# RWKV-7 and Mamba-2 hybrid step: the chunk products of two heads issued in turn, on one Trainium2 core

## The chip, the cores and the metric

The kernel runs on one core of one Trainium2 chip. The metric is device time in microseconds (us). A core has TensorE (PE, with its weight loads shown apart as PEld), VectorE (DVE), ScalarE (ACT), GpSimd (POOL) and SyncE (SP, which here issues the DMAs); each works off its own list of instructions in order, and they meet through semaphores. PSUM, where TensorE writes, has eight banks.

## What is computed

One layer of a streaming encoder for 512 prompt frames (with 16 learned tokens ahead of them) and 64 frames of a running stream, width 2048. Half of the projected columns feed RWKV-7 with 16 heads of 64, the other half Mamba-2; then an output projection, a SwiGLU feed-forward part and a final norm. Cut to the part that matters here:

```python
h = rmsnorm(x, norm_mix_w)
proj = (h @ w_in).astype(F32)
ya, ... = rwkv7_mix(proj[..., :A_COLS], ...)      # r, k, v, decay, a per head of 64
yb, ... = mamba2_mix(proj[..., A_COLS:], ...)
x = x + jnp.concatenate([ya, yb], axis=-1).astype(dtype) @ w_out
h2 = rmsnorm(x, norm_ffn_w)
x = x + (jax.nn.silu(h2 @ ffn_w_gate) * (h2 @ ffn_w_up)) @ ffn_w_down

def step(S, inp):                                 # RWKV-7, one time step
    r_t, w_t, k_t, v_t, kk_t, ka_t = inp
    sa = jnp.einsum('bhij,bhj->bhi', S, kk_t)
    S = S * w_t[:, :, None, :] - sa[..., None] * ka_t[:, :, None, :] + v_t[..., None] * k_t[:, :, None, :]
    return S, jnp.einsum('bhij,bhj->bhi', S, r_t)
```

The kernel doesn't run the recurrence step by step. It cuts time into 10 chunks of 64. In a chunk, products between the (decayed) keys and queries of the 64 steps are taken first, a triangular system is solved, and only a short chain over the chunks is left. The products between keys and queries are what the change is about.

## The kernel before

Work is written out in full when the program is built. A main stream issues the projection as tiles of 128 columns (`in_tile`, line 367, through `product`, line 326): 16 blocks of 128 rows, three products each (high and low halves of the weights) for two halves of the columns of time. Everything else is a task, a Python generator: `go` (206) puts it on a list by priority, and `beat` (215), called three times in each block of the main stream, lets every task go one step whose time has come. Times come from a planner inside the kernel: each engine call is wrapped (`Timed`, 149) and adds an estimated duration to that engine's clock (`tick`, 136). So the order of the instructions on every engine is fixed at build time, by these costs; on the chip only semaphores count. A `yield "P"` gives the turn back until TensorE's time has come, `"VA"` until DVE and ACT are free too.

The 16 heads of RWKV are taken as eight pairs j. The two heads of a pair lie in rows 0 to 63 and 64 to 127 (`hrow`). Per pair:

- `pre_k` and `pre_r` (743, 789) build `KB` and `ST`, from which the gram products are taken. `pre_k` takes two banks of its own for row sums (tile `ss`).
- In `pre_r` (lines 811 to 819) the gram products follow: for each head, for groups of 4, 4 and 2 chunks (`groups`, 787), one bank is taken with `get` (250), one product per chunk goes to it (64 rows, 128 columns out, 128 columns moving, fp32), and `gram_out` (770) is put on the list with priority `PRG` = 1. Tile names begin with `gr`.
- `gram_out` reads one bank: two masked multiplications on DVE, four copies on ACT, then `put` gives the bank back.
- With all six groups read, POOL solves the triangular system in 62 operations (31 steps); `steps` (855) transposes `KB`; `solved` and `applied` (880, 918) apply the solution (tiles `pm`, `pb`, `px`). The gram products of the next pair wait for the `px` products of this one.
- `chain` (984) runs over the 10 chunks (tile `p`, bank 4, priority 0), `post` (1034) normalises.

The tasks of this stage share banks 5, 6 and 7 (line 604 leaves these); the main stream has 0 to 3.

Of the kernel before, what the change touches and what calls it, by code (L numbers as in the profile page):

```python
# [11 lines left out]
F32R = mybir.dt.float32r  # L12
# [5 lines left out]
P = 128  # L18
# [59 lines left out]
PRG = 1  # L78
# [8 lines left out]
def tile_hybrid(ctx, tc, xt, wq, wg, wd, lrw, cst, vec, s0w, s0m, y_out, sh_out, wkv_out, cv_out, sm_out):  # L87
    nc = tc.nc
    V, A, G, PE, SY = nc.vector, nc.scalar, nc.gpsimd, nc.tensor, nc.sync
# [28 lines left out]
    def bank(i, name):  # L118
        return psp.tile([P, 512], F32, tag=f"b{i}", name=name)
# [16 lines left out]
    def tick(e, us):  # L136
        c = cur[0]
        if c.eng != e:
            c.eng, c.base = e, c.t + (0.17 if e == "PE" and c is not main else 0.0)
        end = max(free_at[e], c.base) + us  # L140
        free_at[e] = c.last = end
        if c is not main and not c.aside:
            c.t = max(c.t, end + 0.2)
# [5 lines left out]
    class Timed:  # L149
# [5 lines left out]
        def __getattr__(self, op):  # L155
            f, e = getattr(self.eng, op), self.e

            def call(out, *a, **k):
                r = f(out, *a, **k)  # L159
                part = 0.1 * (out.shape[0] <= 64)  # L160
                if e == "PE":
                    n = out.free_size()
                    tick(e, n / 2400 + 0.0133 if a[1].dtype == F32R else 0.175 if op == "transpose" else max(0.218, 0.15 + n / 1100))
                else:
                    n = (a[0] if op == "tensor_reduce" else out).free_size()
                    s = table.get(a[1]) if op == "activation" else None
                    if s and s != table["now"]:
                        table["now"] = s
                        tick(e, 1.28)
                    if e == "V" and op == "transpose":  # L170
                        us = 0.07 + n / (540 if n > 1000 else 720)
                    elif e == "V" and op in ("tensor_tensor_scan", "reciprocal"):
                        us = 0.07 + n / (480 if op == "tensor_tensor_scan" else 155)
                    elif e == "V":
                        fast = op in ("tensor_copy", "tensor_scalar") and a[0].space == out.space
                        us = 0.07 + n / (960 if not fast else 1920 if not part else 1400) + part * (n > 64)
                        us += 0.06 * (op in SCALED and not isinstance(a[1], float))
                    elif e == "A":
                        us = 0.06 + part + n / 1090 + 0.11 * any(not isinstance(q, float) for q in k.values())
                    else:  # L180
                        us = (0.35 if n < 128 else 0.25) + n / (475 if op == "tensor_tensor" else 1000)
                    tick(e, us)
                return r

            return call

    V, A, G, PE = Timed(V, "V"), Timed(A, "A"), Timed(G, "G"), Timed(PE, "PE")
# [18 lines left out]
    def go(g, prio=5):  # L206
        t = Step()
        t.t, t.g, t.prio = max(now(), cur[0].t), g, prio
        tasks.append(t)
        tasks.sort(key=lambda t: t.prio)  # L210

    def mark(key):
        done[key] = now() if cur[0] is main else cur[0].t
# [14 lines left out]
    def until(*keys, then=None):  # L228
        for k in keys:
            while k not in done:  # L230
                yield then
            cur[0].t = max(cur[0].t, done[k])
        if cur[0].t > now() + SLACK[2]:
            yield then
# [15 lines left out]
    def get():  # L250

        while not spare:
            yield "P"
        b, t = spare.pop(0)
        cur[0].t = max(cur[0].t, t)
        if cur[0].t > now() + SLACK[2]:
            yield "P"
        return b

    def put(b):  # L260
        spare.append((b, cur[0].last + 0.2))
# [410 lines left out]
    R, ses, MVs, st_o = {}, [], [], []  # L672
    hrow = [slice(0, 64), slice(64, 128)]
# [96 lines left out]
    def gram_out(j, h, c0, n, b, pg):  # L770

        yield "VA"
        gb_, st, kx = R["GB"], R["ST"][j % 2][h], 64 * h
        q, m = vrow[h], cc("m3")[:, 64 - 64 * h:192 - 64 * h]
        bc = lambda a: a.unsqueeze(1).broadcast_to([64, n, a.shape[1]])
        V.tensor_tensor(st[q, c0:c0 + n], pg[q, 0:n], bc(m[q]), ALU.mult)
        q, rr = hrow[h], slice(64 - kx, 128 - kx)
        V.tensor_tensor(gb_[q, c0:c0 + n, rr], pg[q, 0:n, rr], bc(m[q, rr]), ALU.mult)
        lo, hi = slice(kx, kx + 32), slice(kx + 32, kx + 64)
        A.copy(R["NX"][lo, c0:c0 + n, :], pg[lo, 0:n, lo])  # L780
        A.copy(R["NX"][hi, c0:c0 + n, :], pg[hi, 0:n, hi])
        A.copy(R["NS"][lo, c0 // 2:(c0 + n) // 2, hi], pg[lo, 0:n:2, hi])
        A.copy(R["NS"][hi, c0 // 2:(c0 + n) // 2, lo], pg[lo, 1:n:2, hi])
        put(b)
        mark(("gram", j, h, c0))

    groups = [(0, 4), (4, 4), (8, 2)]

    def pre_r(j):

        E3 = Eb[:, 0:650].rearrange("p (c t) -> p c t", t=CH + 1)
        Em3 = Em[:, 0:650].rearrange("p (c t) -> p c t", t=CH + 1)
        yield from until("low", ("prek", j), ("Tm", j - 1), then="V")
        KB = R["KB"]
        for h in range(2):
            q, kx = hrow[h], 64 * h
            V.tensor_tensor(KB[q, :, kx:kx + 64], c3(ab)[q], Em3[q, :, 1:CH + 1], ALU.mult)
            yield "V"
            V.tensor_tensor(KB[q, :, 64 - kx:128 - kx], c3(k2)[q], Em3[q, :, 1:CH + 1], ALU.mult)
            yield "V"  # L800
        yield from until(("zr", j), ("cl", j - 2), then="V")
        for h in range(2):
            q, kx, st = hrow[h], 64 * h, R["ST"][j % 2][h]
            V.tensor_tensor(st[q, :, kx:kx + 64], c3(rn)[q], E3[q, :, 0:CH], ALU.mult)
            yield "V"
            V.tensor_tensor(st[q, :, 64 - kx:128 - kx], c3(zr)[q], E3[q, :, 1:CH + 1], ALU.mult)
            yield "V"
        mark(("kb", j))
        go(bonus(j), 2)
        yield from until(*[("px", j - 1, g) for g in range(3)], then="P")  # L810
        for h in range(2):
            q, st = hrow[h], R["ST"][j % 2][h]
            for c0, n in groups:
                b = yield from get()
                pg = bank(b, f"gr{j}{h}{c0}").rearrange("p (c x) -> p c x", x=P)
                for c in range(c0, c0 + n):
                    PE.matmul(pg[:, c - c0, :], KB[q, c, :], st[q, c, :], start=True, stop=True)
                go(gram_out(j, h, c0, n, b, pg), PRG)
                yield "P"
        go(steps(j), PRG)  # L820
        yield from until(*[("gram", j, h, c0) for h in range(2) for c0, _ in groups], then="A")
        mark(("gram", j))

        NX, NN, XT = R["NX"], R["NN"], R["XT"]
        for g in range(1, 3):
            A.copy(NX[:, 10 * g:10 * g + 10], NX[:, 0:10])
        X3 = R["XX"][:, 0:352].rearrange("p (i t) -> p i t", t=32)
        yield "V"
        yield from until(*[("px", j - 1, g) for g in range(3)], then="V")
        V.transpose(NN, NX.rearrange("p c t -> p t c"))  # L830
        yield "P"
        for s in range(31):
            m, r = 31 - s, s // 3 + 1
            tv = XT[:, 0:r * m].rearrange("p (i t) -> p i t", t=m)
            G.tensor_tensor(tv, X3[:, 0:r, s:s + 1].broadcast_to([P, r, m]),
                            NN[:, s + 1:32, s].unsqueeze(1).broadcast_to([P, r, m]), ALU.mult)
            G.tensor_tensor(X3[:, 0:r, s + 1:32], X3[:, 0:r, s + 1:32], tv, ALU.subtract)
        mark(("solve", j))
        yield "P"
        go(solved(j), PRG)  # L840
# [306 lines left out]
    for j in range(NPAIR + 1):  # L1147
        if j < NPAIR:
            go(decay(j), 3)
            go(pre_k(j), 3)  # L1150
            run(f"k{j}", shift_k(j), 1)
            run(f"r{j}", shift_r(j), 1)
        for i in PARK[j]:
            run(f"z{i}", park(i), 1)
        if j < NPAIR:
            go(pre_r(j), 2)
            go(values(j), 2)
            go(chain(j), 0)
        if j:
            run(f"v{j - 1}", shift_v(j - 1), 1)  # L1160
# [834 lines left out]
    for h in range(2):  # L1995
        go(last_norm(h), 2)
        for o in range(NK):
            ps = slot(3, f"e{h}{o}")
            hs = LHS[h]
            x = [[(a[:, hs], c[:, hs]) for a, c in (XT[k] for k in range(4))]]  # L2000
# [161 lines left out]
```

## Time and profile before

| | us |
|---|---|
| median of 3 runs | 2800.07 |
| lowest and highest | 2793.95, 2803.86 |
| the profiled execution | 2797.02 |
| its span, first to last instruction | 2795.1 |
| PE, DVE, ACT, POOL busy | 2658.5, 2187.0, 1405.9, 385.8 |

An fp32 product is shown as two MATMUL records with a weight load each, so the 160 gram products are 320 records. Tiles are named without their numbers: `gr` are the gram banks, `mk`, `mr`, `mv`, `mz`, `mB`, `mC`, `mx` the tiles of the projection. Nearly all lines read L159, since every engine call goes through one helper. "Chain" is the chain of work that ended last, followed back from the end of a stretch. PEclk is the granted clock of TensorE as a share of its upper level.

### The profile page before, as it was taken

The numbers are of one execution on the slowest core, as the hardware profiler recorded it, in microseconds if no ns is written. First come the engines' busy times: TensorE is split into PE (matmuls) and PEld (weight loads), VectorE is DVE, ScalarE is ACT, GpSimd is POOL, SyncE is SP. The second block draws the span as 40 slices with busy tenths as digits, with TensorE's granted clock in tenths as the row PEclk, the third lists the DMA queues.
The fourth block names the chain that finished last, engine by engine and source line by source line (L and its number), as shares of the span: only waits on it lengthen the run. The fifth ranks groups of instructions, "written<-read, shape, count | busy, mean of one in ns | idle before, by whom it ended". The sixth has DMA issues, their size and how long they took to land.

```text
span 2795.1 us, 51964 instructions
## 1 busy us (share of the span) xinstructions
PE 2658.5 (95%) x19236; PEld 2587.9 (93%) x19236; DVE 2187.0 (78%) x4216; ACT 1405.9 (50%) x3013; POOL 385.8 (14%) x673
## 2 busy tenths in 40 slices
PE   8998899989999999989999999999999979999897
PEld 8888789989998989989999999999999979989897
DVE  7675787878778674678988888898888668878785
ACT  5645566556655443454445445444544334444344
POOL 3234324444401110220000000000000000000004
PEclk9999799999999999999999999999999989999899
DMA  5421122222122244343434344443434666373523
GB/s 180 173 74 50 47 70 65 69 57 77 56 86 91 97 150 122 119 150 121 150 128 158 129 144 144 141 150 128 158 128 150 211 213 207 117 229 95 182 76 110
DMA packets 196462, 349.57 MB, mean 125 GB/s; under 512 B 26097, under 2 KB 102001, under 8 KB 196081
## 3 DMA queue, kind: packets, MB, share of 16 engines
q1 hardware_dynamic: 196208, 346.26, 38.6%
q8 instruction: 151, 2.47, 0.4%
q14 instruction: 103, 0.84, 0.1%
HBM read 281.13 MB, written 65.06 MB: 124 GB/s over the span
## 4 chain that ended last, share of the span: by engine, by line
PE 77%; DVE 5%; ACT 4%; DMA 4%; POOL 3%; issue 2%; SPq 0%; DVEq 0%; ACTq 0%; POOLq 0%
PE y L159 14%; PE a L159 14%; PE r L159 14%; PE x L159 7%; PE mwo L159 7%; DVE mem L159 5%; POOL mem L159 3%; PE mx L159 3%; ACT mem L159 3%; PE mv L159 3%; PE mk L159 2%; PE mr L159 2%; DMA ffm<-pd 2%; PE mz L159 2%; PE p L159 2%
## 5 line engine op out<-in xcount | busy, mean ns | idle before, releaser
L159 ACT CAST memr<-mem 128x512 fp32r<-128x512 f32 (+2 forms) x1230 | 714.3, 585 | 925.3 <-PE y L159 210.0
L159 DVE TENSOR_TENSOR memr<-mem,memr 128x512 fp32r<-128x512 f32 (+2 forms) x1076 | 692.3, 648 | 282.5 <-ACT memr L159 275.4
L159 DVE TENSOR_TENSOR mem<-mem 128x576 f32<-128x576 f32 (+9 forms) x1016 | 695.8, 701 | 36.0 <-DMA mem<-x1d 26.1
L159 POOL TENSOR_TENSOR mem<-mem 128x84 f32<-128x84 f32 (+28 forms) x583 | 337.1, 579 | 2256.0 <-ACT mem L159 1591.0
L159 ACT ACTIVATE mem<-mem 64x64 f32<-64x64 f32 (+12 forms) x413 | 217.0, 533 | 175.1 <-DVE mem L159 155.5
L159 PE MATMUL r<-ffm,memr 128*128 128x288 f32 x1348 | 206.0, 299 | 17.3 <-DVE memr L159 12.7
L159 PE MATMUL a<-ffm,memr 128*128 128x288 f32 x1328 | 201.9, 299 | 12.5 <-ACT memr L159 9.9
L159 PE MATMUL mwo<-memr 128*128 128x288 f32 x1536 | 210.4, 298 | 0.0
L159 PE MATMUL y<-ffm,memr 128*128 128x288 f32 x1356 | 203.4, 297 | 7.2 <-DMA ffm<-pd 7.2
L159 PE MATMUL y<-memr 128*128 128x288 f32 x1352 | 203.0, 296 | 6.5 <-DVE mem L159 5.5
L159 PEld LDWEIGHTS mwo<-memr 128*128 128x128 f32 x1536 | 205.9, 189 | 3.0 <-issue 2.5
L159 PEld LDWEIGHTS r<-ffm,memr 128*128 128x128 f32 x1348 | 190.5, 192 | 19.5 <-DVE memr L159 13.0
L159 PE MATMUL x<-memr 128*128 128x288 f32 x1352 | 201.5, 295 | 0.0
L159 PE MATMUL a<-memr 128*128 128x288 f32 x1352 | 200.3, 295 | 1.2 <-DVE memr L159 1.2
L159 PEld LDWEIGHTS a<-ffm,memr 128*128 128x128 f32 x1328 | 187.1, 191 | 14.2 <-ACT memr L159 10.1
L159 PE MATMUL r<-memr 128*128 128x288 f32 x1352 | 199.1, 294 | 0.0
L159 PEld LDWEIGHTS y<-ffm,memr 128*128 128x128 f32 x1356 | 189.6, 190 | 8.1 <-DMA ffm<-pd 5.0
L159 PEld LDWEIGHTS y<-memr 128*128 128x128 f32 x1352 | 189.0, 189 | 7.4 <-issue 5.9
L159 PEld LDWEIGHTS a<-memr 128*128 128x128 f32 x1352 | 187.3, 189 | 1.4 <-DVE memr L159 1.4
L159 PEld LDWEIGHTS x<-memr 128*128 128x128 f32 x1352 | 187.8, 188 | 0.0
L159 PEld LDWEIGHTS r<-memr 128*128 128x128 f32 x1352 | 186.2, 188 | 0.0
L159 PE MATMUL mk<-memr 128*128 128x296 f32 x768 | 125.2, 313 | 4.6 <-DVE mem L159 4.4
(184 smaller groups left out, 4055.8 us busy)
## 6 DMA issues: line engine op xcount, KB each, us to landing
mem<-in_wg SPq DMA_DIRECT2D x176, 512.0 KB, 3.4
mem<-in_wq SPq DMA_DIRECT2D x268, 256.0 KB, 2.7
mem<-in_wd SPq DMA_DIRECT2D x128, 320.0 KB, 3.1
pd<-mem SPq DMA_DIRECT2D x280, 144.0 KB, 2.0
memr<-pd SPq DMA_DIRECT2D x80, 288.0 KB, 6.3
ffm<-pd SPq DMA_DIRECT2D x60, 288.0 KB, 6.6
mem<-lrd SPq DMA_DIRECT2D x16, 320.0 KB, 3.7
mem<-in_xt SPq DMA_DIRECT2D x16, 296.0 KB, 5.9
```

The source lines that it names most:

```text
L159: r = f(out, *a, **k)
```

## The change

The loop over heads goes inside. For each group two banks are taken first, one per head; then chunk by chunk the product of head 0 and that of head 1 are issued in turn, each from its own 64 rows into its own bank; then both evacuations are put on the list, and the turn is given back once per group. The planner's cost of a product with 64 rows of contraction is halved. These are the only two edits.

```diff
-                    tick(e, n / 2400 + 0.0133 if a[1].dtype == F32R else 0.175 if op == "transpose" else max(0.218, 0.15 + n / 1100))
+                    tick(e, n / 2400 + 0.0133 if a[1].dtype == F32R else 0.175 if op == "transpose" else max(0.218, 0.15 + n / 1100) * (0.5 if a[0].shape[0] == 64 else 1))
@@ pre_r
-        for h in range(2):
-            q, st = hrow[h], R["ST"][j % 2][h]
-            for c0, n in groups:
-                b = yield from get()
-                pg = bank(b, f"gr{j}{h}{c0}").rearrange("p (c x) -> p c x", x=P)
-                for c in range(c0, c0 + n):
-                    PE.matmul(pg[:, c - c0, :], KB[q, c, :], st[q, c, :], start=True, stop=True)
-                go(gram_out(j, h, c0, n, b, pg), PRG)
-                yield "P"
+        for c0, n in groups:
+            bs = []
+            for h in range(2):
+                bs.append((yield from get()))
+            pg = [bank(bs[h], f"gr{j}{h}{c0}").rearrange("p (c x) -> p c x", x=P) for h in range(2)]
+            for c in range(c0, c0 + n):
+                for h in range(2):
+                    q = hrow[h]
+                    PE.matmul(pg[h][:, c - c0, :], KB[q, c, :], R["ST"][j % 2][h][q, c, :], start=True, stop=True)
+            for h in range(2):
+                go(gram_out(j, h, c0, n, bs[h], pg[h]), PRG)
+            yield "P"
```

## Rows read from the trace of the kernel before

**Rows 1.** The page: busy us, share, instructions; granted clock in 40 slices

```profile
PE 2658.5 (95%) x19236; PEld 2587.9 (93%) x19236; DVE 2187.0 (78%) x4216; ACT 1405.9 (50%) x3013; POOL 385.8 (14%) x673
...
PEclk9999799999999999999999999999999989999899
```

**Rows 2.** Busy time by stretch, around pairs 2 and 6, and the feed-forward part

```profile
core 0: us, PE busy (x) PEld busy (x) DVE busy (x) ACT busy (x) POOL busy (x), PEclk, DMA share, GB/s
...
315.00:394.00 79.00, 73.39 (x440) 66.64 (x439) 61.72 (x133) 48.48 (x130) 28.39 (x64) 0.79 0.14 38
634.00:712.00 78.00, 76.57 (x560) 72.89 (x559) 63.80 (x137) 48.91 (x132) 30.14 (x64) 1.00 0.24 71
1050.00:2795.00 1745.00, 1677.89 (x12465) 1667.55 (x12464) 1400.50 (x2567) 811.30 (x1559) 67.72 (x60) 0.98 0.45 146
```

**Rows 3.** The chain that ended last, 156 to 770 us, shares by engine and tile

```profile
by line: POOL mem L159 14.8%; DVE mem L159 11.6%; ACT mem L159 9.9%; PE mv L159 9.9%; PE mk L159 8.2%; PE mr L159 7.8%; PE p L159 7.2%; issue 5.6%; PE mz L159 4.1%; PE gr L159 4.1%; ACT L159 3.4%; PE pb L159 2.4%; PE mB L159 1.9%; ACT memr 
```

**Rows 4.** PE's groups by shape: rows*columns, shape, count, busy us, mean ns, idle before

```profile
L159 PE MATMUL gr<-mem 64*128 64x128 f32 x320 | 53.6, 313 | 2.3 <-ACT mem L159 2.1
```

**Rows 5.** The chain's pieces: start us, us on the chain, what, records

```profile
165.36 2.00 PE gr L159 x8
...
315.15 2.08 PE gr L159 x8
...
642.77 0.64 PE gr L159 x4
...
644.28 1.09 PE gr L159 x8
```

**Rows 6.** Instructions in order of time, pair 5: start us, us, engine, what, count

```profile
562.00 1.17 PE L159 MATMUL gr<-mem 64*128 64x128 f32 x12
...
563.69 1.16 PE L159 MATMUL gr<-mem 64*128 64x128 f32 x8
```

**Rows 7.** Busy by stretch of `gr` alone (PE, PEld, DVE, ACT): pairs 0 to 2

```profile
156.00:246.00 90.00, 7.31 (x41) 6.06 (x42) 5.86 (x12) 5.17 (x24) 0.89 0.22 67
246.00:315.00 69.00, 5.88 (x40) 4.74 (x40) 5.78 (x12) 5.18 (x24) 1.00 0.22 63
315.00:394.00 79.00, 10.39 (x41) 8.92 (x41) 5.86 (x12) 5.17 (x24) 0.79 0.14 38
```

**Rows 8.** Waits of PE and PEld, 156 to 780 us: total us, times, longest

```profile
PE p L159 <- DVE mem L159: 15.6, 21, 4.2
...
PEld gr L159 <- ACT mem L159: 5.7, 10, 2.5
PEld gr L159 <- issue: 5.1, 29, 0.3
```

**Rows 9.** Instructions in order of time, gram products and evacuations of pair 6

```profile
634.15 1.16 PE L159 MATMUL gr<-mem 64*128 64x128 f32 x8
...
636.16 0.70 PE L159 MATMUL ss<-mem 128*128 128x320 f32 x2
...
637.61 1.16 PE L159 MATMUL gr<-mem 64*128 64x128 f32 x8
...
639.88 0.70 PE L159 MATMUL ss<-mem 128*128 128x320 f32 x2
...
640.86 0.95 ACT L159 COPY mem<-gr 32x128 f32<-32x128 f32 x4 [0.73 <-PE mr L159]
...
652.59 0.81 ACT L159 COPY mem<-gr 32x64 f32<-32x64 f32 x4 [0.97 <-DVE mem L159]
```

**Rows 10.** POOL's group of the solve, 156 to 770 us: count, busy us, mean ns

```profile
L159 POOL TENSOR_TENSOR mem<-mem 128x84 f32<-128x84 f32 (+23 forms) x496 | 230.9, 465 | 365.5 <-DVE mem L159 327.2
```

**Rows 11.** Busy time by stretch, two stretches at a low granted clock

```profile
228.00:240.00 12.00, 6.72 (x32) 6.75 (x33) 4.74 (x13) 2.76 (x7) 3.55 (x13) 0.57 0.09 23
314.00:349.00 35.00, 30.00 (x111) 24.36 (x112) 25.15 (x53) 24.03 (x69) 7.58 (x21) 0.51 0.03 10
```

**Rows 12.** Instructions in order of time, PE alone: the idle time before, and for whom

```profile
233.28 2.31 PE L159 MATMUL pm<-mem 128*128 128x33 f32 x10 [7.85 <-ACT mem L159]
```

## The prediction, made before the change ran

> **What bounds the kernel now.** I read the page's shares first: TensorE (PE) is busy 95% of the span, VectorE (DVE) 78%, ScalarE (ACT) 50%, and the granted clock is below its upper level in places [rows 1]. Then the busy time by stretch [rows 2]. The change touches only the stretch from 156 to 723 us, where the gram products of the eight RWKV pairs run; from 1050 us on the program is the feed-forward part, and nothing there is edited. Inside the stretch the picture is uneven: around pair 6 (634 to 712 us) PE is busy 76.57 of 78 us, around pair 2 (315 to 394) 73.39 of 79 at a mean clock of 0.79. So PE is nearly packed, but not the only limit. The chain of waits says what the rest is: of the chain that ended last in 156 to 770 us, 14.8% lies on POOL (the triangular solve that follows the gram products of a pair), 11.6% on DVE, 9.9% on ACT, and 4.1% on the gram products themselves [rows 3]. The RWKV pairs are a loop (gram, solve, apply, next pair's gram) beside a stream of projection matmuls, and the end of the stage is set now by one and now by the other.
>
> **The change, part by part.**
>
> *The products.* There are 160 gram products, each shown as two MATMUL records, so 320 records, and theirs is the only shape with 64 active rows [rows 4]. They come in bursts: per pair four of 8 records and two of 4. On the chain a burst of 8 stands with 1.09 us and one of 4 with 0.64 [rows 5]. The difference, 0.45 us for 4 records, makes 0.90 us of pure work in a burst of 8, so each burst also pays an edge of 0.19 us for coming and going. Before, a pair costs 4 x 1.09 + 2 x 0.64 = 5.64 us.
>
> What two heads cost when their 64 rows differ is visible once in the trace of before, by accident of the schedule: in pair 5 the last group of head 0 (4 records) is followed directly by the first of head 1 (8 records). The 12 records take 1.17 us from the first start to the last end; a burst of 8 records of one head right behind it takes 1.16 [rows 6]. So the four records of the other head cost 0.01 us instead of 0.45: the two halves of the array worked at the same time. In the change every burst is of that kind, 8 + 8, 8 + 8 and 4 + 4 records. I take 1.10 us for the two larger and 0.65 for the smaller: 2.85 us for a pair. PE thus saves 2.79 us per pair, 22.3 us for eight. Where the clock was at its lower level the bursts were longer (10.39 us busy in the stretch of pair 2 against 5.88 in that of pair 1 [rows 7]); half of that excess of 4.5 us and of pair 0's 1.4 us (7.31 against 5.88) is saved too if the clock does the same again, 3.0 us. That makes 25.3 us, the upper bound of what PE can give back.
>
> *What of it is on the path.* The chain holds 4.1% of 614 us = 25.2 us of gram products [rows 3], a little under half of the 53.6 us that they are busy [rows 4]. With the order of everything else kept, shortening them by 2.79/5.64 = 49% takes 12.4 us off this chain, and the time can't fall by more than what its longest chain loses. The rest of the saving lies where the chain runs over POOL, DVE or ACT, and there it makes idle PE time. What can lift it above 12.4 is that the order is not kept (next point); the ends are therefore 0 and 25.3, and I take the chain's 12.4, since it is the row that weighs the saving by what was late.
>
> *The planner's cost.* The tick of a product with 64 contraction rows is halved: from 0.15 + 128/1100 = 0.266 to 0.133 us, 20 per pair, 2.66 us. That agrees with the 2.79 above, so the written-out order will fit the chip about as it did. Projection matmuls and all later tasks move up by it. Most of this is the same order earlier; local reorderings cost or gain unknown amounts. The nearest rows are the waits of PE for chain steps in this stage, where the order was ahead of the chip: 15.6 us in 21 times [rows 8]. I give it 0 and plus or minus 6 in the range.
>
> *The banks.* Each group now takes two banks before its first product, out of the three that the tasks of this stage share. The added wait sits in front of head 1's first product (and head 0's, which is issued with it); behind it on PE's queue stand the projection matmuls, and who waits for those is the split of the next weights on ACT and DVE. Before, weight loads of gram products waited 5.7 us for ACT in 10 places, and 5.1 us without a cause in the profile in 29 places, which is the edge again [rows 8]. Half as many bursts that each wait for the later of two banks: between -2.8 us (half of 5.7) and +5.7 (each burst waits for both, as long as now). I take 0. What it could do to the loop is a rival below.
>
> *The evacuation.* Per pair DVE spends 5.8 and ACT 5.2 us on reading the gram banks [rows 7]; the instructions are the same in number and size, only the order of the heads alternates, and each `gram_out` still waits for its own bank. Both heads' banks become ready together, 1.1 us after the start, when before one was. Nothing is removed there. In pair 6 the last copy ends at 653.40, 19.3 us after the first product [rows 9], while PE needs 5.64 of them: the phase is long because evacuations are queued among other DVE and ACT work. That speaks against a gain in the loop. The Trainium skill, TensorEngine Tiling (Array Packing), section Performance Considerations, says the same as a rule: packing speeds up TensorE and not the reading of PSUM, which may become the bound. The trace agrees as far as 5.8 us of DVE against 2.85 of PE goes; what it would give is the second rival.
>
> *Turns.* The loop yields three times per pair and no longer six, so the tasks behind it get three turns fewer; a turn is a pair of projection matmuls, and they are issued anyway. Nothing.
>
> Sum: the profiled execution took 2797.02 us (span 2795.1), 3.05 under the median of the runs, 2800.07. 2797.02 - 12.4 = 2784.6, which is 2787.7 on the median's footing.
>
> **The rivals.**
>
> *No overlap.* If heads in turn don't overlap (the one place in rows 6 had them as blocks of 4 and 8, not in turn), only three edges per pair go: 3 x 0.19 x 8 = 4.6 us, of which by the chain's share (25.2/53.6) 2.2 us count: 2798. Against it: rows 6 show four records hidden one after the other, not only the first.
>
> *The evacuation and the solve keep the pace.* If in every pair the loop is set by the copies and POOL, the saving counts only where PE was packed and gram was on the chain throughout, pairs 6 and 7 (5.6 us): 2794.5. For it: the 14.8% of POOL and the 19.3 us phase. Against it: the chain passes through gram bursts of pairs 0 and 2 as well, there of 2.00 and 2.08 us at the lower clock [rows 5].
>
> *Slower: the bank pair.* With three banks and two per group, the second group holds the third bank empty until a bank of the first is read. In pair 6 a bank of a burst was occupied from 637.61 to 641.81, 4.2 us [rows 9]. If each of the two later groups of a pair starts that much later, the solve starts 8.4 us later. It counts where POOL's solve is on the chain, in about three of the eight pairs: 14.8% of 614 us is 91 us, and the solves are 230.9 us busy for eight pairs [rows 10], 29 us each, so about three are on it. 3 x 8.4 = 25.2 us lost, 12.4 gained: +12.8, 2812.9. It decides once the groups lose more than 12.4/3 = 4.1 us per pair, one occupied bank. Against it: before, one bank at a time, the gram already shared the banks with the row-sum products of the next pair (at 636.16 and 639.88 in rows 9), so that the six bursts were spread over 16 us anyway.
>
> *The clock.* The stretch 228 to 240 us ran at 0.57 of the full clock, so at the lower level (1.2 GHz) for most of it, and 314 to 349 at 0.51 [rows 11]; in the first, PE had stood idle for 7.85 us before its product at 233.28 [rows 12]. One such stretch more or less, with its 6.72 us of PE work at half pace, is worth about 3 us. This widens the range by 3 at either end and decides no case alone.
>
> **How the numbers follow.** About 0.3% (8.4 us) is what a measurement of this kernel can tell from no change, so faster means under 2791.7. The forecast (8.4 to 25 us gained) gets 0.60: the overlap is in the trace, and the chain carries half of the saving. Evacuation and solve keep the pace: 0.22; no overlap: 0.07; both stay within 0.3%. The bank pair: 0.11. So faster 0.60, same 0.29, slower 0.11. The range begins at 2800.07 - 25.3 - 3 = 2772 (everything PE saves, and one clock stretch fewer) and ends at 2806, which takes in both cases without change and the adverse side of order or banks (6 us over the median); the bank pair lies beyond.
>
> **What would show it.** In the profile after: gram records start in pairs of the two heads, a full burst of 16 takes 1.1 to 1.2 us and the gram tile's busy time in PE falls from 53.6 to 24 to 28 us (wrong if it stays above 45: no overlap). The time from the first gram product of a pair to its last evacuation stays near 19 us or falls; if it grows by over 4 us, the bank pair is at work. The chain's share of gram in this stage falls to about 2%, and the feed-forward part keeps its length. If PE's idle time in the stage grows by as much as the bursts shrink, the evacuation rival is right. The forecast is wrong if the stage ends less than 8 us earlier although the bursts have halved.

## The result, and the profile after

The changed kernel takes 2825.86 us (median of 4 runs, 2822.36 to 2830.18) against 2800.27 for the kernel before: a ratio of 1.0091, 95% interval 1.0076 to 1.0105. It is 25.6 us slower, where 12.4 us faster was forecast, and outside the stated range. The two executions that were profiled lie 33.3 us apart (spans of 2828.4 and 2795.1), somewhat more than the medians. The page of after, busy time and granted clock (to [rows 1]):

```profile
PE 2655.8 (94%) x19236; PEld 2589.6 (92%) x19236; DVE 2185.3 (77%) x4216; ACT 1402.8 (50%) x3011; POOL 390.4 (14%) x673
...
PEclk9999899888999999999999999999999989999899
```

The products do what they were meant to do. Instructions of pair 6 in order of time (to [rows 6, 9]):

```profile
644.19 1.16 PE L159 MATMUL gr<-mem 64*128 64x128 f32 x16
...
649.58 1.16 PE L159 MATMUL gr<-mem 64*128 64x128 f32 x16
...
659.58 1.62 ACT L159 COPY mem<-gr 32x64 f32<-32x64 f32 x8 [1.11 <-PE mv L159]
```

A burst of 16 records takes the 1.16 us that one of 8 took before: the second head is free. The busy time of the gram products in the group by shape (to [rows 4]) falls from 53.6 to 33.6 us (24 to 28 had been expected), but the idle time before them rises from 2.3 to 10.8:

```profile
L159 PE MATMUL gr<-mem 64*128 64x128 f32 x320 | 33.6, 323 | 10.8 <-ACT mem L159 6.9 <-DVE mem L159 3.8
```

Where the time came from is seen when the RWKV stage is taken by itself, from 156 us to the last product of the last pair's chain (tile `p`). The rows of that tile give its first and last start, before and then after:

```profile
L159 PE MATMUL p<-mem x320: 217/275/476, 251.9 to 839.3; 128*128 128x64 f32 x160
```

```profile
L159 PE MATMUL p<-mem x320: 217/275/475, 248.5 to 869.2; 128*128 128x64 f32 x160
```

The last product starts 29.9 us later. From there to the end of the span it is 1955.8 us before (2795.1 - 839.3) and 1959.2 after (2828.4 - 869.2). So nine tenths of the 33.3 us lie in the RWKV stage, and everything behind the last chain follows at a nearly fixed distance. The last 1748 us of the two kernels are alike too, first before, then after (columns as in [rows 2]):

```profile
1047.00:2795.00 1748.00, 1680.89 (x12488) 1670.55 (x12486) 1402.30 (x2571) 813.00 (x1561) 67.72 (x60) 0.98 0.45 146
```

```profile
1080.00:2828.00 1748.00, 1680.72 (x12473) 1669.45 (x12471) 1401.82 (x2567) 810.59 (x1558) 66.90 (x60) 0.98 0.45 146
```

The stage itself, before and then after:

```profile
156.00:839.50 683.50, 635.84 (x4407) 596.99 (x4407) 524.88 (x1128) 402.34 (x1075) 238.80 (x513) 0.94 0.22 65
```

```profile
156.00:869.50 713.50, 631.52 (x4408) 597.24 (x4407) 524.18 (x1128) 403.33 (x1077) 242.98 (x513) 0.91 0.21 62
```

DVE, ACT and POOL do the same work. PE is busy 4.3 us less although 20 us of gram went, because it ran at the lower clock for longer: a mean of 0.94 over 683.5 us is about 82 us at the lower level, 0.91 over 713.5 about 128. PE's idle time rises from 47.7 to 82.0 us (length less busy). In the chain of 156 to 804 us (to [rows 3]) POOL's share rises from 14.8 to 28.3% and DVE's from 11.6 to 18.9%, and the path lies less on PE's products:

```profile
by line: POOL mem L159 28.3%; DVE mem L159 18.9%; ACT mem L159 11.8%; issue 9.8%; PE p L159 4.0%; PE mv L159 3.5%; PE pb L159 3.0%; PE mk L159 2.8%; ACT L159 2.4%; PE mz L159 2.2%; PE mr L159 2.0%; DVE memr L159 2.0%; ACT memr L159 1.9%; PE 
```

That share doesn't measure the loss, though: in the loop in turn with the cost left whole (an experiment below), whose last chain product comes only 6.9 us later than before, at 846.2, POOL has 34.8% of the chain of 156 to 846.2 us.

Two places at which PE stands. The waits of PE in the stage (to [rows 8]) show the products of the solution (`pm`) at the head, 16.8 us on DVE, where before they waited 7.8 us on ACT and 2.4 on DVE. Before, then after:

```profile
PE pm L159 <- ACT mem L159: 7.8, 1, 7.8
...
PE pm L159 <- DVE mem L159: 2.4, 2, 1.8
```

```profile
PE pm L159 <- DVE mem L159: 16.8, 4, 7.2
PE p L159 <- DVE mem L159: 14.2, 20, 3.6
PE gr L159 <- ACT mem L159: 6.9, 4, 3.3
```

And in pair 2 the second bank is missing in the middle of a burst; instructions in order of time:

```profile
321.98 0.49 PE L159 MATMUL gr<-mem 64*128 64x128 f32 x2
321.99 1.28 ACT L159 ACT_TABLE_LOAD   x1
323.28 1.43 ACT L159 ACTIVATE mem<-mem 128x640 f32<-128x640 f32 x3
324.74 1.93 ACT L159 COPY mem<-gr 32x128 f32<-32x128 f32 x8
...
325.75 2.08 PE L159 MATMUL gr<-mem 64*128 64x128 f32 x14 [3.28 <-ACT mem L159]
```

Head 0's first product (two records) runs in the free bank; head 1's needs the one that ACT reads only from 324.74 on, behind a table load and other work. PE stands for 3.28 us with the chain's products queued behind, and the stretch that follows is at the lower clock level (1.2 GHz) nearly throughout:

```profile
323.00:341.00 18.00, 11.23 (x51) 9.48 (x52) 9.10 (x23) 8.06 (x31) 0.00 (x0) 0.53 0.06 19
```

The kernel before was at the lower level in its pair 2 as well (0.51 [rows 11]), and neither place is the loss by itself: the loop with the cost left whole has both (below).

### The profile page after: what moved, and what is told of

The parts are those of the page before. It is cut to its first block, busy times and chain, and to the rows that moved or that the text cites. A ratio compares the mean times of both kernels' runs of the same rounds, so it can differ in the third digit from the quotient of the medians.

```text
span 2828.4 us, 51951 instructions
## 1 busy us (share of the span) xinstructions
PE 2655.8 (94%) x19236; PEld 2589.6 (92%) x19236; DVE 2185.3 (77%) x4216; ACT 1402.8 (50%) x3011; POOL 390.4 (14%) x673
## 4 chain that ended last, share of the span: by engine, by line
PE 70%; DVE 8%; POOL 7%; ACT 5%; DMA 4%; issue 3%; SPq 0%; DVEq 0%; ACTq 0%; POOLq 0%
PE y L159 14%; PE a L159 14%; PE r L159 14%; PE x L159 7%; POOL mem L159 7%; PE mwo L159 7%; DVE mem L159 6%; ACT mem L159 3%; PE mz L159 2%; PE mx L159 2%; DMA ffm<-pd 2%; PE me L159 2%; PE mv L159 1%; PE p L159 1%; PE mk L159 1%
## 5 line engine op out<-in xcount | busy, mean ns | idle before, releaser
L159 PE MATMUL r<-ffm,memr 128*128 128x288 f32 x1348 | 206.3, 299 | 17.2 <-DVE memr L159 12.8
L159 PE MATMUL a<-ffm,memr 128*128 128x288 f32 x1328 | 201.6, 298 | 13.4 <-ACT memr L159 10.3
L159 PEld LDWEIGHTS r<-ffm,memr 128*128 128x128 f32 x1348 | 190.9, 192 | 19.3 <-DVE memr L159 13.0
```

## The experiments

Theories at the outset: the two banks held at once, or the planner's shifted order ("replanning"). Four kernels separate the two edits of the change.

**Only the cost.** The loop stays head by head:

```diff
-  ... max(0.218, 0.15 + n / 1100))
+  ... max(0.218, 0.15 + n / 1100) * (0.5 if a[0].shape[0] == 64 else 1))
```

> The loop of before, head by head with one bank at a time; only the planner's cost of a gram product is halved. Bank theory (the loss of 25.6 us comes from TensorE standing in a burst until the second bank is read, up to 3.5 us at a time, and from the low clock that follows): within 8 us of before, 2792 to 2808, gram busy 50 to 56 us. Replanning theory (a changed cost shifts the order written out, and that alone moves the time by tens of us): 2815 to 2835, as far off as the changed kernel.

Measured: 2828.07 us, ratio 1.0098 (1.0069 to 1.0126). The whole loss appears without any overlap and without a second bank. The chain's last product is as late as in after:

```profile
L159 PE MATMUL p<-mem x320: 217/275/473, 255.1 to 866.9; 128*128 128x64 f32 x160
```

**Only the loop.** The new loop with the cost left whole, so the diff above taken back from after:

> The loop of after (two banks, heads in turn), the planner's cost of a gram product left whole. Bank theory: slow all the same, 2812 to 2835, with several waits of over 1 us inside bursts. Replanning theory (the halved cost is at fault): 2780 to 2800, since the overlap then comes without a wrong cost.

Measured: 2805.48 us, 1.0023 (1.0012 to 1.0034). Both theories missed the time: not slow as the bank theory wanted, and not faster than before. Yet the waits inside bursts are there, four of them of over 1 us, the 3.28 us of pair 2 among them, and `pm` waits long as well:

```profile
318.62 0.48 PE L159 MATMUL gr<-mem 64*128 64x128 f32 x2
...
322.38 2.07 PE L159 MATMUL gr<-mem 64*128 64x128 f32 x14 [3.28 <-ACT mem L159]
```

```profile
PE pm L159 <- DVE mem L159: 11.4, 5, 3.6
PE pm L159 <- ACT mem L159: 7.2, 1, 7.2
```

So the two places shown in after don't make its loss. Two banks and turns without the changed cost come out 6 us slower, with the gain of the overlap already in that figure; what the order costs without the overlap is measured further down.

**A small push.** The cost of a gram product times 0.9, nothing else changed from before (`0.9` in place of `0.5` in the diff above):

> The kernel before with the planner's cost of a gram product times 0.9 (0.239 in place of 0.266 us), nothing else. It measures what a small push to the planner does by itself. Bank theory: 2795 to 2806. Replanning theory: more than 8 us off in either direction, below 2792 or above 2809.

Measured: 2829.34 us, 1.0107 (1.0087 to 1.0127). A cost changed by 0.027 us per product, 0.5 us per pair, moves the kernel by 29 us. That settles it against the bank theory as the main cause, and it says more: the time depends on the order that the planner happens to write.

**One bank at a time, groups outside.**

```diff
-        for h in range(2):
-            for c0, n in groups:
+        for c0, n in groups:
+            for h in range(2):
                 b = yield from get()
                 ...
                 yield "P"
```

> The groups go outside and the heads inside as in after, but each head of a group takes one bank, issues its products and yields, as before; cost whole. So the order of the evacuations is that of after, without two banks held at once and without overlap by design. Bank theory: 2792 to 2808. Replanning theory: any value between 2780 and 2835. If the order of the heads among the evacuations is what costs: above 2812.

Measured: 2821.77 us, 1.0080 (1.0058 to 1.0102). Slower without a second bank and without a changed cost, as replanning allows; that the order of the heads among the evacuations costs would also give it, so this run alone tells little.

**What the overlap is worth at a fixed order.** If every push gives another order, the overlap must be taken away without moving anything. Head 1's products are taken from the same 64 rows as head 0's:

```diff
-                    q = hrow[h]
-                    PE.matmul(pg[h][:, c - c0, :], KB[q, c, :], R["ST"][j % 2][h][q, c, :], start=True, stop=True)
+                    o = P * c if h == 0 else P * min(c, NC - 2) + 64
+                    ops = [a[hrow[0]].rearrange("p c x -> p (c x)")[:, o:o + P] for a in (KB, R["ST"][j % 2][0])]
+                    PE.matmul(pg[h][:, c - c0, :], *ops, start=True, stop=True)
```

The lists of instructions of the compute engines are the same as in the kernel compared with, in the same order. First against after:

> The changed kernel with the same order of instructions on every engine, but head 1's gram products also taken from rows 0 to 63 (head 0's keys, shifted by half a chunk), so the two heads can't overlap; head 1's results are left out by that. Theory that the overlap is worth what PE saves: 2826 + 20 to 25 = 2846 to 2851. Theory that the stage is a loop whose copies and solve set the pace: 2826 to 2836. If the overlap itself does harm (clock, banks): below 2818. Gram bursts of 16 records 2.0 us in all three.

Measured: 2834.19 us, 1.0112 (1.0096 to 1.0129) over before, where after has 1.0091: 0.0021, or 5.9 us, with an uncertainty of about 0.0022. That is inside the range of the loop theory. A burst of 16 now takes 2.05 us, and the gram products are busy 51.45 us in the stage against 33.31 in after (timeline of pair 6; then busy time of `gr` alone in the stage):

```profile
653.54 2.05 PE L159 MATMUL gr<-mem 64*128 64x128 f32 x16
```

```profile
156.00:874.50 718.50, 51.45 (x316) 44.97 (x314) 44.95 (x96) 41.58 (x192) 0.91 0.21 61
```

Then against the loop with the cost left whole:

> The same for the two-bank loop with the planner's cost left whole (2805.5): same order of instructions as that kernel, head 1's products from head 0's rows, so no overlap. Overlap worth all that PE saves: 2826 to 2830. Loop theory: 2805 to 2815. Harm by the overlap: below 2800.

Measured: 2823.15 us, 1.0071 (1.0056 to 1.0086), where the overlapped kernel has 1.0023: 0.0048, or 13.4 us, with an uncertainty of about 0.0019. It lies between the ranges of the loop theory and of the whole saving. So the overlap helps, by 13 us in one order and by 6 (not clear of nothing) in the other. Against after PE's gram time is 18.1 us longer (51.45 against 33.31), and in the second comparison 21.3 (54.73 against 33.42); about a third and two thirds of that arrive. Busy time of `gr` alone in the stage, without and with overlap, cost left whole:

```profile
156.00:864.40 708.40, 54.73 (x318) 47.70 (x317) 44.87 (x96) 41.56 (x192) 0.91 0.21 62
```

```profile
156.00:846.20 690.20, 33.42 (x318) 26.59 (x318) 44.86 (x96) 41.43 (x192) 0.93 0.22 64
```

The two kernels without overlap also give the price of the orders by themselves: 1.0112, 31 us, for the order of the change, and 1.0071, 20 us, for that of the new loop with the cost left whole. Together with the 28 us of the cost alone they don't add up: each edit, and both together, make another order.

**One direction, or a draw?** Is the halved cost bad because it is too low, so that the order runs ahead of the chip, or is any cost but that of before a new draw? The same one-line edit with other factors, in the loop before ("one head") and in the new loop ("in turn"):

> The kernel before with the planner's cost of a gram product times 1.1. Theory that a cost that is too low does the harm (the order is then ahead of the chip): 2795 to 2806. Theory that the order of before is a good draw and any push redraws it: above 2809, as with 0.9.

> The kernel before, cost of a gram product times 1.01: a push of 0.05 us per pair. Theory of the draw: the order differs in places and the time moves by more than 5 us, most likely up, as with 0.9 and 1.1. Theory of the cost: within 4 us of before.

> The one-head loop, cost times 0.95. If the time follows the cost: between before (2800) and 0.9 (2829), 2810 to 2820. If a draw: 2800 to 2835, above the two-head loop at the same cost by 6 to 13 us if only the overlap differed.

> The one-head loop, cost times 0.7. If the time follows the cost: 2826 to 2832, since 0.5 and 0.9 gave 2828 and 2829. If a draw: 2800 to 2835.

> The same loop, cost times 0.7. Theory of the draw: 2790 to 2830. Theory of the cost: between 0.5 (2826) and 0.9 (2803), 2810 to 2820.

> Two banks, heads in turn, cost times 0.8. Theory of the draw: 2790 to 2830, not ordered with its neighbours 0.7 and 0.9. Theory of the cost: between these two.

> Two banks, heads in turn, cost times 0.85. On a curve: 2804 to 2810, between 0.8 (0.32% over before) and 0.9 (0.11%). If a draw: 2795 to 2826.

> The two-bank loop, heads in turn, cost of a gram product times 0.9. Theory of the low cost: between the 2805 of cost 1 and the 2826 of cost 0.5, near 2810. Theory of the draw: anything from 2795 to 2835, with no order by cost.

> Two banks, heads in turn, cost times 0.95. If the six costs of this loop so far (0.5, 0.7, 0.8, 0.9, 1.0, 1.1 of the cost: 0.91, 0.64, 0.32, 0.11, 0.23, 0.52% over before) lie on a curve: 2800 to 2807. If each is a draw: 2795 to 2826.

> Two banks, heads in turn, the planner's cost of a gram product times 1.1. Theory of the draw (each cost gives another order, the times of a loop scatter by 10 us and more, and the overlap gives 6 to 13 us beneath it): 2790 to 2825, about 10 us under the draws of the one-head loop on average. Theory of the cost (too low is slow, too high is fast): 2795 to 2806.

Measured, as ratio to before (the intervals are 0.001 to 0.003 to either side):

| factor on the cost | one head | in turn |
|---|---|---|
| 0.5 | 1.0098 | 1.0091 (the change) |
| 0.7 | 1.0085 | 1.0064 |
| 0.8 | | 1.0032 |
| 0.85 | | 1.0055 |
| 0.9 | 1.0107 | 1.0011 |
| 0.95 | 1.0139 | 1.0051 |
| 1 | 1 (before) | 1.0023 |
| 1.01 | 1.0035 | |
| 1.1 | 1.0050 | 1.0052 |

Six points of the loop in turn had looked like a curve with its lowest place near 0.9; the two points put between them (0.85 and 0.95) lie 0.34% above the line between their neighbours. In the other loop 0.95 is the slowest and 1 the fastest of seven. There is no order by cost, so the theory that a cost too low does all the harm falls and that of the draw stands; that the low costs are slow on the whole (0.5 and 0.7 are the slowest in turn) isn't ruled out. The ranges given for the draw were wide, and one of them was missed, 0.95 with one head (2840.25); 0.8 in turn lies between 0.7 and 0.9, as the theory of the cost had it. Each kernel's time follows its last chain product, over all eighteen kernels at 1949 to 1960 us from it to the end of the span. The smallest push, a factor of 1.01, ends the chain at 852.6, and 0.95 at 879.9:

```profile
L159 PE MATMUL p<-mem x320: 217/275/476, 252.9 to 852.6; 128*128 128x64 f32 x160
```

```profile
L159 PE MATMUL p<-mem x320: 217/275/474, 250.9 to 879.9; 128*128 128x64 f32 x160
```

With 1.01 the lists of PE are equal up to pair 4 (483 us on the chip before); there two bursts of the gram stand one pair of projection products later, and from there on the lists differ. Before, then with 1.01:

```profile
481.21 2.04 PE L159 MATMUL mv<-memr 128*128 128x296 f32 x12
483.18 1.16 PE L159 MATMUL gr<-mem 64*128 64x128 f32 x8
484.26 0.54 PE L159 MATMUL mv<-memr 128*128 128x296 f32 x2
484.73 0.71 PE L159 MATMUL gr<-mem 64*128 64x128 f32 x4
485.37 0.81 PE L159 MATMUL mv<-memr 128*128 128x296 f32 x4
```

```profile
482.67 2.30 PE L159 MATMUL mv<-memr 128*128 128x296 f32 x14
484.91 1.16 PE L159 MATMUL gr<-mem 64*128 64x128 f32 x8
485.99 0.53 PE L159 MATMUL mv<-memr 128*128 128x296 f32 x2
486.52 0.71 PE L159 MATMUL gr<-mem 64*128 64x128 f32 x4
487.16 0.81 PE L159 MATMUL mv<-memr 128*128 128x296 f32 x4
```

At equal factors (0.5, 0.7, 0.9, 0.95, 1, 1.1) the loop in turn stands to the other by -0.07, -0.21, -0.96, -0.88, +0.23 and +0.02%, on average -0.31%, 9 us faster: the size of the overlap measured at a fixed order, but with a scatter of 0.5% between single pairs, so this mean by itself isn't clear of nothing. No kernel tried beats the one before; the nearest is the loop in turn with a factor of 0.9, at 1.0011 (1.0001 to 1.0021).

## Why the prediction was wrong

- *The overlap* was right, and read from the one accident in the trace of before. 16 records take 1.16 us (1.10 was taken for start to next start), and without overlap 2.05. The "no overlap" rival is out. The busy time was put too low (24 to 28 us, measured 33.6): bursts that a wait breaks or that run at the lower level take longer, 14 records 2.08 us in pair 2.
- *What of it is on the path*: 12.4 us forecast, 13.4 and 5.9 measured at a fixed order. Those are two other orders than the one whose chain was read, so the likeness of 12.4 and 13.4 is in part luck. Read in their own chains of the kernels without overlap (5.5% of 708.4 us and 4.0% of 718.1, shortened by the 39 and 35% that PE saved there), the same method gives 15.2 and 10.1 us, within the uncertainty of both. So the chain's share was a fair measure, and the bound of 25.3 was not approached. The two chains, first with the cost left whole, then with the cost of the change:

```profile
by line: POOL mem L159 25.7%; DVE mem L159 16.4%; ACT mem L159 8.0%; issue 7.4%; PE p L159 6.0%; PE gr L159 5.5%; PE mk L159 5.1%; PE mx L159 5.0%; PE mv L159 4.4%; PE mB L159 2.3%; PE pb L159 2.3%; DVE memr L159 2.1%; ACT L159 1.8%; PE mr 
```

```profile
by line: POOL mem L159 25.3%; DVE mem L159 14.3%; ACT mem L159 8.2%; issue 7.8%; PE mk L159 6.3%; PE mv L159 6.2%; PE p L159 5.5%; PE gr L159 4.0%; PE mr L159 2.9%; PE pb L159 2.5%; ACT L159 2.3%; PE mz L159 2.0%; PE mB L159 1.8%; PE mx L15
```

- *The planner's cost* is the step that failed. It said that the order "will fit the chip about as it did" and gave local reorderings 0, plus or minus 6 us. Measured, the halved cost alone costs 28 us, and one of 0.9 costs 29. The new loop's turns and banks, put at "Nothing" and 0, failed in the same way: at the old cost and without overlap it is 20 us slower, and no run separates these two. With the order of the change and no overlap it is 31 us. The term was too small by a factor of about five, and it was centred wrongly: of seven costs in the old loop that of before is the fastest, the others lie 0.35 to 1.39% above. The order of before is a good draw among those tried, and a push to a good draw loses more often than it gains; the prediction took it for an average one.
- *The banks*: between -2.8 and +5.7 us were given. In the rows that the prediction used, the waits of the gram products' weight loads, the time on the banks' readers rose from 5.7 us (all on ACT) to 12.9 (9.5 on ACT, 3.4 on DVE), by 7.2, a little outside, and some of it stands inside a burst, where the chain's products are blocked. That is a cost of the new loop, but the cost-only kernel is as slow without it, and the new loop at the old cost has it and is 6 us slower.
- *The rival of the bank pair* forecast the right side and half of the size (+12.8, 2812.9), for the wrong reason. It needed the gram phase to grow by 4.1 us per pair. From the first product to the end of the last ACT copy the eight pairs take 155.8 us before in sum and 167.3 after, 1.4 us per pair, and in the cost-only kernel, as slow as after, 147.2; in pair 6 the phase even shrank, from 19.3 us [rows 9] to 17.0 (644.19 to 661.20).
- *The evacuation and the solve*: part of this rival is there: at a fixed order 13.7 of the 18.1 us that PE saved, and 9.2 of the 21.3, came back as its idle time. Its sign was that PE's idle time grows by as much as the bursts shrink; it grew by 34 us where they shrank by 20, and the rival has no term that makes the kernel slower. POOL's doubled share of the chain is no sign for it, since the loop with the cost left whole has more of it and is 20 us faster than after.
- *The clock* was given 3 us either way. The stage holds about 46 us more at the lower level. The cost-only kernel has the same products as before in its stage, which is 27.6 us longer: PE is busy 15.4 us longer with them (651.0 against 635.6) at a mean clock of 0.91 against 0.94, and idle 12.2 longer. So about half of that loss shows as slower products. How much of it the clock caused I can't say: low stretches follow stalls of PE, and they make the chain's products slower (four records of `p` take 0.66 us before the stall in pair 2 and 1.09 behind it), so they are effect and cause at once. No run held the clock apart.
- The chain rows told that POOL, DVE and ACT set the pace in part; what was missed is that the end follows the last chain product at a nearly fixed distance. Lateness inside the loop is partly made up, or added to, later: the first gram product comes 15.4 us later than before in pair 5, 10.0 in pair 6 and 16.6 in pair 7, and the last chain product 29.9. In the loop with the cost left whole it is 16.1 us late in pair 7 and the last chain product 6.9. So 13 of the 30 us in after arise behind the last pair's first gram product. Pairs 5 and 7, before, then after:

```profile
551.98 1.16 PE L159 MATMUL gr<-mem 64*128 64x128 f32 x8
...
712.45 1.16 PE L159 MATMUL gr<-mem 64*128 64x128 f32 x8
```

```profile
567.41 0.48 PE L159 MATMUL gr<-mem 64*128 64x128 f32 x2
...
729.06 1.16 PE L159 MATMUL gr<-mem 64*128 64x128 f32 x16
```

Open: which orders are good, and why. PE stands longer before the `pm` products than before (10.2 us in all) in each of the seventeen other kernels, 10.7 to 21.7 us; but it does so for 18.6 us in the loop with the cost left whole, which is only 6 us slower. No single place was shown to carry the 25 us.

## What to carry to other kernels

Where the order of instructions comes out of a planner, a change to a cost or to the number of turns is a second change, here larger than the one intended (28 us against 6 to 13): give it a range of its own, from a run with the cost moved and nothing else, and don't centre it at zero before it is known whether the present order is an average one. Measure the thing itself at a fixed order (here by pointing both heads at the same rows), and measure the order by several small pushes. In a loop with a fixed tail, read the time from the last turn of the loop.

## What the runs showed of the hardware

Two streams of fp32 products on different halves of the array's rows run fully beside each other here, 16 records in 1.16 us against 2.05 on the same half, even when the groups are issued as blocks one behind the other (12 records in 1.17 us [rows 6]). What the overlap can't pass is a semaphore: the product of head 1 that waits for its bank stops head 0's next ones as well, 3.28 us in the place shown.
